# An encoder layer on one core: the reciprocal square roots of its norms move from twelve VectorE instructions to two GpSimd instructions

## The chip, the cores and the metric

The kernel runs on one core of a Trainium2 chip. The metric is the device time of one execution in microseconds (us), smaller is better. Five engines work side by side, each through its own queue of instructions in order: TensorE (PE in the profile, with PEld for its weight loads), VectorE (DVE), ScalarE (ACT), GpSimd (POOL) and SyncE (SP), which here issues the transfers. They wait for one another through semaphores.

## The reference

One layer of an encoder is applied, with the same weights, to two batches: 2048 and 1024 tokens of width 1024. The token mixing has a Fourier half (a two-dimensional DFT) and a half of gating heads (a 128x128 mixing matrix per head); the channel mixing is a gated up-projection to 2 x 2816, a convolution of width 3 over positions, GELU and a down-projection. Around them stand RMS norms, and these are what the change is about:

```python
def _rmsnorm(x, g):
    xf = x.astype(jnp.float32)
    y = xf * lax.rsqrt(jnp.mean(xf * xf, axis=-1, keepdims=True) + EPS)
    return (y * g.astype(jnp.float32)).astype(x.dtype)

def _trunk(x, ...):
    m = _token_mixer(_rmsnorm(x, pre_mix_norm[l]), ...)      # inside: v = _rmsnorm(v, sgu_norm) per head
    x = x + _rmsnorm(m, post_mix_norm[l])
    c = _channel_mixer(_rmsnorm(x, pre_ffn_norm[l]), ...)
    x = x + _rmsnorm(c, post_ffn_norm[l])
```

All arrays are float32, and so are the results.

## The kernel before

The products are done in float32 by splitting each operand into a high part (fp32r, a copy by ScalarE) and the rest (a subtraction by VectorE or GpSimd: `split`), and by three passes over the parts. The large projections use Strassen's scheme in Winograd's form: seven products `p0` to `p6` of twelve matmuls each, made from sums of blocks (`sums`, on GpSimd: s0 to s3) and split operands w0 to w6. The seven products of two tiles of 128 rows are one step.

The program is a list of slots. `at(slot, order, fn)` puts a piece of work into a slot; inside a slot the loads come first, then the preparation for later slots, the matmuls, and what takes the products out of PSUM. At the end all slots are run through in order, and so each engine's queue is fixed: an instruction that waits holds up all that stands behind it on its engine.

The stages, in the order of the slots, are: twelve chunks of 128 tokens times the Fourier columns (`Fourier`, each chunk one slot; tiles xT, xh, xl, pz, z) while the weights of the gating heads get ready (wr, sog); twelve steps of gating heads (`Gate`, seven slots each; names end in g); twelve more Fourier chunks; twelve mixes (`Mix`, four slots each: position DFT with the tables th and tl, output projection, norm, residual, and the norm before the up-projection); 66 steps of the up-projection (`Up`; names end in u); and 36 steps of the down-projection in three groups (`Down`; names end in d), the last of which adds the residual and stores y.

The norms need one number per token (or per token and head), the reciprocal square root of a mean of squares. ScalarE sums the squares into a small tile (ss or vs), 128 partitions by one, two or eight columns. `Rsqrt` turns it into the factor: a first guess by integer operations on the bits of the float, and three rounds of Newton's iteration, together twelve VectorE instructions (L107 to L118). There are 62 of these: r1 for the input's norm (12, into the tile rall; used by `Fourier.out` on VectorE and by `Gate.gelu` on ScalarE), rv per gating step (12, eight columns; used by `vnorm` on VectorE), r2 after each mix (12; used by `residual` on VectorE), r3 before the up-projection (10 of two columns in the mixes and 4 of one column in the first steps of the up-projection; used by ScalarE), r4 in the last down group (11; used by `yout` on VectorE), and rl at the very end.

`Vec` wraps VectorE: behind each large instruction one step of a queued chain is issued, so that a chain is spread over the work of the next slots. Chains with `wait=None` (r1, r2, two-column r3, rl) are issued at once in one piece, since `Rsqrt.__init__` asks for `col(0)`, and `col` issues all that is still queued. The others start in the queue, and whatever is left of them is issued when a user asks for the factor. In the gating steps rv is queued at slot s+6, and its user `vnorm` stands at s+8.

Of the kernel before, what the change touches and what calls it, by code (L numbers as in the profile page):

```python
# [11 lines left out]
F32 = mybir.dt.float32  # L12
# [5 lines left out]
D = 1024  # L18
# [7 lines left out]
# 128-token tiles in processing order: (batch, parity, kt) -> (direct tile, mirrored tile)  # L26
# [7 lines left out]
def tile_trunk(  # L34
# [46 lines left out]
    # Chains of small operations on the vector engine are queued and issued one by one behind  # L81
    # its large operations, so that it doesn't wait for the latency of each.
    queued = []

    class Vec:
        def __getattr__(self, name):
            f = getattr(nc.vector, name)

            def issue(*args, **kw):
                f(*args, **kw)  # L90
                if queued:
                    queued.pop(0)()

            return issue

    vec = Vec()

    class Rsqrt:
        """(ss / n + EPS) ** -0.5 by Newton's iteration, on [128, k]."""

        def __init__(self, ss, k, n, name, wait=None, out=None):
            v = S.tile([128, k], F32, tag=f"nv{k}", name=f"{name}_v")
            yv = S.tile([128, k], F32, tag=f"ny{k}", name=f"{name}_y") if out is None else out
            q = S.tile([128, k], F32, tag=f"nq{k}", name=f"{name}_q")
            tt, ts, stt = nc.vector.tensor_tensor, nc.vector.tensor_scalar, nc.vector.scalar_tensor_tensor
            ops = [lambda: None] * (wait or 0) + [
                lambda: ts(v, ss, 0.5 / n, 0.5 * EPS, op0=ALU.mult, op1=ALU.add),  # L107
                lambda: ts(q.bitcast(I32), v.bitcast(I32), 1, None, op0=ALU.arith_shift_right),
                # the first guess, negative: each of the three iterations changes the sign
                lambda: ts(  # L110
                    yv.bitcast(I32), q.bitcast(I32), -1, 0x5F3759DF - (1 << 22) - (1 << 31),
                    op0=ALU.mult, op1=ALU.add,
                ),
            ]
            ops += 3 * [
                lambda: tt(q, yv, yv, op=ALU.mult),
                lambda: tt(q, q, v, op=ALU.mult),
                lambda: stt(yv, q, -1.5, yv, op0=ALU.add, op1=ALU.mult),  # L118
            ]
            self.done = False  # L120
            queued.extend(ops + [self.end])
            self.y = yv
            if wait is None:
                self.col(0)

        def end(self):
            self.done = True

        def col(self, i):
            while not self.done:  # L130
                queued.pop(0)()
            return self.y[:, i : i + 1]
# [14 lines left out]
    # The program is a list of slots; in each one the loads and splits for later slots are  # L147
    # issued before the products, and what takes the products out of PSUM after them.
# [6 lines left out]
    # Strassen's scheme in Winograd's form for [C11 C12; C21 C22] = [A11 A12; A21 A22] [B11 B12; B21 B22]:  # L155
    # the right operands of the seven products in the order of the products
    B11, B21, T4, T2, T3, T1, B22 = range(7)

    def right_sums(t1, b11, b12, b21, b22, last=True):
        """t1 = T1 and, in place, b12 = T3, b11 = T2, b21 = T4."""  # L160
        nc.gpsimd.tensor_tensor(t1, b12, b11, op=ALU.subtract)
        nc.gpsimd.tensor_tensor(b12, b22, b12, op=ALU.subtract)
        nc.gpsimd.tensor_tensor(b11, b12, b11, op=ALU.add)
        if last:
            nc.gpsimd.tensor_tensor(b21, b11, b21, op=ALU.subtract)

# [28 lines left out]
    class Step:  # L195
        """Two tiles of 128 rows times the right operands of a stage: seven products."""
# [106 lines left out]
    def fold(k):  # L303
        """The rows of the Fourier columns' weights times the DFT over a group's channels."""
        if k % 2 == 0:
            for e in range(2):
                wf[e].append(unit(f"wf{e}{k}", F32R, (128, 2, 512)))
        pf = bank(f"pf{k}")
        for g in range(4):
            nc.tensor.matmul(  # L310
                pf[:, g * 128 : (g + 1) * 128],
                lhsT=wft[k // 2][:, g, (k % 2) * 128 : (k % 2) * 128 + 128],
                rhs=rd, start=True, stop=True,
            )
# [18 lines left out]
    class Stat:  # L333
        """The norm's factors of two chunks of 128 tokens."""
# [11 lines left out]
        def scale(self):  # L346
            pr = self.pr
            ss = S.tile([128, 2], F32, tag="ss1", name=f"ss1_{pr}")
            for j in range(2):
                nc.scalar.activation(self.xc[j], self.xc[j], AF.Square, accum_out=ss[:, j : j + 1])  # L350
            self.r = Rsqrt(ss, 2, D, f"r1_{pr}", out=rall[:, 2 * pr : 2 * pr + 2])

    class Fourier:
        """The Fourier columns of one chunk of 128 tokens."""
# [30 lines left out]
    class Heads(Stage):  # L385
        """The weights of the gating heads; the halves of the columns are v and u."""

        def load(self, q):
            """Blocks 11, 21, 12, 22."""
# [24 lines left out]
    class Gate(Step):  # L414
        """The gating heads of two chunks of 128 tokens."""
# [46 lines left out]
        def vscale(self):  # L462
            self.rv = Rsqrt(self.vs, 8, 128, f"rv{self.nm}", 0)
# [79 lines left out]
    # The Fourier columns come before and after the gating heads, so that each one's  # L543
    # weights get ready while the other's are in use.
# [7 lines left out]
    def begin():  # L552
# [17 lines left out]
        stats[0].scale()  # L570

# [13 lines left out]
    for pr in range(12):  # L585
        if 0 < 2 * pr < NB:
            at(2 * pr - 2, LOAD if pr > 1 else MM + 0.1, stats[pr].load)
            at(2 * pr - 1, PREP + 0.3, stats[pr].scale)
    at(10, STORE, wf_store)
# [13 lines left out]
    for pr in range(12):  # L603
# [3 lines left out]
        if 2 * pr >= NB:  # L607
            at(s - 5, LOAD, stats[pr].load)
            at(s - 3, OUT + 0.5, stats[pr].scale)
        at(s + 1, OUT + 0.2, g.vout, 0)  # L610
        at(s + 5, OUT + 0.2, g.vout, 1)
        at(s + 6, OUT + 0.2, g.vscale)
# [11 lines left out]
    # ------------------------------------------------------------------ position DFT, projection out  # L624
# [49 lines left out]
    def product(o0, o1, aparts, wparts, first=True, last=True):  # L674
        """o0|o1 += the sum over parts of a.T @ w, in three passes."""
# [13 lines left out]
    # the tiles of d_ff: three groups of (first half, second half)  # L689
# [27 lines left out]
    class Side:  # L717
        """z[s] + z[s + S/2], or their difference, of one batch."""
# [21 lines left out]
    class Mix:  # L740
        """One tile of 128 frequencies and the tile of their mirror images."""
# [87 lines left out]
        def centre(self):  # L829
            """The frequency S/2, which has no mirror image."""  # L830
# [74 lines left out]
        def norm(self):  # L905
# [7 lines left out]
            self.r2 = Rsqrt(ss, 2, D, f"r2{nm}")  # L913
# [31 lines left out]
        def rs_again(self, i):  # L945
            vec.tensor_add(self.ss3[:, 0:1], self.ss3[:, 0:1], self.ss3[:, 1:2])
            self.r3 = Rsqrt(self.ss3[:, 0:1], 1, D, f"r3{self.nm}{i}", 0)
# [88 lines left out]
    for i, m in enumerate(mixes):  # L1036
# [26 lines left out]
        at(s + 3 + 4 * (i == 11), OUT + 0.7, m.norm)  # L1063
        at(s + 4 + 6 * (i == 11), OUT + 0.5, m.residual)
# [22 lines left out]
    # ------------------------------------------------------------------ up-projection, conv, gate  # L1087
# [4 lines left out]
    class Up(Step):  # L1092
        """Gate and up of one tile of d_ff; the columns are the even and the odd positions."""
# [116 lines left out]
    # ------------------------------------------------------------------ down-projection  # L1210
# [7 lines left out]
    class Down(Step):  # L1218
        """Two tiles of tokens, one group of d_ff; the columns are the halves of the output's."""
# [31 lines left out]
        def post(self, j):  # L1251
            """The last two steps: as little as possible comes after their last products."""
# [38 lines left out]
        def scale(self):  # L1291
            self.r = Rsqrt(self.ss, 2, D, f"r4{self.nm}", 0)
# [202 lines left out]
```

## Time and profile before

| | |
|---|---|
| median of 3 runs | 2967.51 us (2967.39 to 2967.82) |
| span of the profiled execution | 2965.6 us |
| PE busy | 2722.0 us (92%) |
| DVE busy | 2639.4 us (89%), 3995 instructions |
| ACT busy | 1214.2 us (41%) |
| POOL busy | 1548.3 us (52%), 918 instructions |
| mean granted TensorE clock | 0.966 of full |

The page has no time of the profiled execution other than its span, from the first to the last instruction. A busy share is a mean over stages in which different engines are full, so the rows further down are by stretches and by single steps. The time of an instruction in a row includes what it waits for after its start, as for a port that another engine holds; the time it waits ahead of its start for another instruction's result stands in brackets, with the instruction that ended the wait.

### The profile page before, as it was taken

The numbers are of one execution on the slowest core, as the hardware profiler recorded it, in microseconds if no ns is written. First come the engines' busy times: TensorE is split into PE (matmuls) and PEld (weight loads), VectorE is DVE, ScalarE is ACT, GpSimd is POOL, SyncE is SP. The second block draws the span as 40 slices with busy tenths as digits, with TensorE's granted clock in tenths as the row PEclk, the third lists the DMA queues.
The fourth block names the chain that finished last, engine by engine and source line by source line (L and its number), as shares of the span: only waits on it lengthen the run. The fifth ranks groups of instructions, "written<-read, shape, count | busy, mean of one in ns | idle before, by whom it ended". The sixth has DMA issues, their size and how long they took to land.

```text
span 2965.6 us, 35147 instructions
## 1 busy us (share of the span) xinstructions
PE 2722.0 (92%) x11930; PEld 2192.1 (74%) x11930; DVE 2639.4 (89%) x3995; ACT 1214.2 (41%) x2317; POOL 1548.3 (52%) x918
## 2 busy tenths in 40 slices
PE   8788899988779999998999998999998999999997
PEld 7576777877667777786787776777776887887775
DVE  7988977789799999999999999999999668669999
ACT  5334443454454444444443444344344232224332
POOL 2633411345555555556555556445455337668766
PEclk9899999999889999999999999999998999999999
DMA  8435449456772323252222143122124464566665
GB/s 305 162 130 181 161 167 331 152 187 206 220 241 85 111 96 107 95 175 79 85 86 86 70 151 93 70 80 85 64 96 145 126 204 158 163 202 210 204 191 180
DMA packets 279572, 440.39 MB, mean 149 GB/s; under 512 B 22304, under 2 KB 171296, under 8 KB 279392
## 3 DMA queue, kind: packets, MB, share of 16 engines
q1 hardware_dynamic: 279392, 438.16, 44.1%
q8 instruction: 93, 1.52, 0.2%
q14 instruction: 87, 0.71, 0.1%
HBM read 302.81 MB, written 135.28 MB: 148 GB/s over the span
## 4 chain that ended last, share of the span: by engine, by line
DVE 36%; PE 26%; issue 13%; ACT 3%; DMA 2%; POOL 1%; SPq 0%; DVEq 0%; ACTq 0%; POOLq 0%
DVE t1u L90 8%; DVE t0u L90 4%; PE p3u L234 3%; PE p5u L234 3%; PE p4u L234 3%; DVE uu L90 2%; DVE c21u L90 2%; PE p5d L234 2%; PE p6d L234 2%; PE p4d L234 2%; PE p0d L234 2%; PE p3d L234 2%; PE p2d L234 2%; PE p1d L234 2%; DVE sox L90 2%
## 5 line engine op out<-in xcount | busy, mean ns | idle before, releaser
L1158 POOL TENSOR_TENSOR t0u<-t0u,t1u 128x1024 f32<-128x1024 f32 x66 | 160.0, 2424 | 395.0 <-ACT t0u L1157 394.9
L234 PE MATMUL p3u<-sox,w3u 128*128 128x512 f32 x792 | 208.5, 403 | 22.7 <-DVE w3u L90 21.0
L234 PE MATMUL p0u<-sox,w0u 128*128 128x512 f32 x792 | 201.1, 404 | 25.0 <-ACT w0u L135 13.9
L234 PE MATMUL p6u<-sox,w6u 128*128 128x512 f32 x792 | 200.4, 397 | 9.6 <-DVE w6u L90 9.6
L234 PE MATMUL p2u<-sox,w2u 128*128 128x512 f32 x792 | 198.1, 399 | 10.0 <-ACT w2u L135 5.6
L136 POOL TENSOR_TENSOR w4u<-s2u,w4u 128x512 fp32r<-128x512 f32 x65 | 101.2, 1557 | 202.4 <-ACT w4u L135 198.4
L1157 ACT ACTIVATE t0u<-t0u 128x1024 f32<-128x1024 f32 x66 | 70.1, 1062 | 326.8 <-DVE t0u L90 324.1
L234 PEld LDWEIGHTS p3u<-sox,w3u 128*128 128x128 f32 x792 | 147.1, 191 | 74.0 <-DVE w3u L90 42.3
L234 PE MATMUL p5u<-sox,w5u 128*128 128x512 f32 x792 | 195.0, 395 | 7.4 <-DVE w5u L90 3.8
L234 PEld LDWEIGHTS p0u<-sox,w0u 128*128 128x128 f32 x792 | 154.1, 196 | 61.6 <-ACT w0u L135 16.0
L234 PE MATMUL p4u<-sox,w4u 128*128 128x512 f32 x792 | 192.1, 391 | 2.5 <-DVE w4u L90 2.1
L234 PE MATMUL p1u<-sox,w1u 128*128 128x512 f32 x792 | 191.5, 390 | 2.3 <-DVE w1u L90 2.3
L234 PEld LDWEIGHTS p6u<-sox,w6u 128*128 128x128 f32 x792 | 146.4, 189 | 52.8 <-DVE w6u L90 22.3
L234 PEld LDWEIGHTS p2u<-sox,w2u 128*128 128x128 f32 x792 | 148.5, 191 | 48.9 <-DVE w2u L90 11.2
L234 PEld LDWEIGHTS p5u<-sox,w5u 128*128 128x128 f32 x792 | 150.3, 191 | 41.6 <-DVE w5u L90 5.9
L1109 ACT ACTIVATE t1u<-c21u,cbt,cwt 128x512 f32<-128x512 f32 x66 | 53.9, 817 | 298.3 <-DVE c21u L90 289.1
L90 DVE TENSOR_TENSOR w6u<-s3u,w6u 128x512 fp32r<-128x512 f32 x66 | 155.8, 2360 | 22.1 <-ACT w6u L135 22.1
L234 PEld LDWEIGHTS p4u<-sox,w4u 128*128 128x128 f32 x792 | 149.2, 189 | 34.5 <-DVE w4u L90 2.5
L234 PEld LDWEIGHTS p1u<-sox,w1u 128*128 128x128 f32 x792 | 148.5, 188 | 33.9 <-DVE w1u L90 3.2
L90 DVE SCALAR_TENSOR_TENSOR t1u<-c21u,cwt,t1u 128x511 f32<-128x511 f32 (+4 forms) x220 | 164.7, 772 | 3.1
L242 ACT COPY ud<-p0d 128x512 f32<-128x512 f32 x34 | 20.0, 588 | 346.4 <-PE p0d L234 346.4
L90 DVE SCALAR_TENSOR_TENSOR t1u<-c22u,cwt,t1u 128x511 f32<-128x511 f32 (+4 forms) x220 | 141.5, 668 | 3.1
(363 smaller groups left out, 7724.5 us busy)
## 6 DMA issues: line engine op xcount, KB each, us to landing
ra0u<-w_up SPq DMA_DIRECT2D x66, 512.0 KB, 4.5
ra1u<-w_up SPq DMA_DIRECT2D x66, 512.0 KB, 5.3
g_d<-t0u SPq DMA_DIRECT2D x66, 512.0 KB, 2.9
srx<-xo_d SPq DMA_DIRECT2D x42, 512.0 KB, 6.6
xT<-xT SPq DMA_DIRECT2D x24, 512.0 KB, 8.0
xc<-xc SPq DMA_DIRECT2D x24, 512.0 KB, 5.4
zz<-z_d SPq DMA_DIRECT2D x48, 256.0 KB, 5.5
xr<-x_po SPq DMA_DIRECT2D x24, 512.0 KB, 6.0
```

The costliest lines, as they stand in the source:

```text
L90: f(*args, **kw)
L136: (eng or vec).tensor_tensor(l, src, h.bitcast(F32), op=ALU.subtract)
L234: nc.tensor.matmul(ps, lhsT=w[:, a, k], rhs=op[k][:, b], start=k == 0 and a + b == 0, stop=k == n - 1 and a == 1)
L242: nc.scalar.copy(self.u, p[0])
L1109: nc.scalar.activation(t[:, i], p, AF.Identity, bias=cbt[:, ti : ti + 1], scale=cwt[:, ti, 1:2])
L1157: nc.scalar.activation(ga, ga, AF.Gelu_apprx_tanh)
L1158: nc.gpsimd.tensor_tensor(ga, ga, self.t[1], op=ALU.mult)
```

## The change

`Vec` and its queue go; `vec` is VectorE itself. `Rsqrt` issues two GpSimd instructions at once: mean and epsilon in one affine step, and a power of -0.5 with the exponent from a constant tile. Since they are issued where `Rsqrt` is made, the calls move to slots of their own: `Stat.root` one slot behind the squares (or at the end of the same slot), `vscale` from s+6 to the end of s+7, `Mix.rs2` to the head of the slot of its user `residual`. No other instruction of PE, ScalarE or SyncE is moved.

```diff
@@
-    class Vec:
-        def __getattr__(self, name):
-            f = getattr(nc.vector, name)
-            def issue(*args, **kw):
-                f(*args, **kw)
-                if queued:
-                    queued.pop(0)()
-            return issue
-    vec = Vec()
+    vec = nc.vector
+    power = C.tile([128, 8], F32, name="power")
+    nc.gpsimd.memset(power, -0.5)
@@ class Rsqrt
-            tt, ts, stt = nc.vector.tensor_tensor, nc.vector.tensor_scalar, nc.vector.scalar_tensor_tensor
-            ops = [lambda: None] * (wait or 0) + [
-                lambda: ts(v, ss, 0.5 / n, 0.5 * EPS, op0=ALU.mult, op1=ALU.add),
-                lambda: ts(q.bitcast(I32), v.bitcast(I32), 1, None, op0=ALU.arith_shift_right),
-                lambda: ts(
-                    yv.bitcast(I32), q.bitcast(I32), -1, 0x5F3759DF - (1 << 22) - (1 << 31),
-                    op0=ALU.mult, op1=ALU.add,
-                ),
-            ]
-            ops += 3 * [
-                lambda: tt(q, yv, yv, op=ALU.mult),
-                lambda: tt(q, q, v, op=ALU.mult),
-                lambda: stt(yv, q, -1.5, yv, op0=ALU.add, op1=ALU.mult),
-            ]
...
+            nc.gpsimd.tensor_scalar(v, ss, 1.0 / n, EPS, op0=ALU.mult, op1=ALU.add)
+            nc.gpsimd.tensor_tensor(self.y, v, power[:, :k], op=ALU.pow)
@@ where they are called
+            at(2 * pr - 1, OUT + 0.5, stats[pr].root)
...
+            at(s - 2, OUT + 0.5, stats[pr].root)
...
-        at(s + 6, OUT + 0.2, g.vscale)
+        at(s + 7, OUT + 0.6, g.vscale)
...
+        at(s + 4 + 6 * (i == 11), PREP - 0.1, m.rs2)
```

On VectorE, in the eighth gating step, this stood before the change ahead of the fifth product's operand of the next step (w4g is an operand that TensorE waits for; v2g with rvg_y is `vnorm`):

```order
L90 TENSOR_TENSOR v2g_2758<-ug_2712,p1g_2735 128x512
L116 TENSOR_TENSOR rvg_q<-rvg_y 128x8
L90 COPY gTg_2769<-ptg_2748 128x8x64
L117 TENSOR_TENSOR rvg_q<-rvg_q,rvg_v 128x8
L90 COPY gTg_2769<-ptg_2753 128x8x64
L118 SCALAR_TENSOR_TENSOR rvg_y<-rvg_q,rvg_y 128x8
L116 TENSOR_TENSOR rvg_q<-rvg_y 128x8
L117 TENSOR_TENSOR rvg_q<-rvg_q,rvg_v 128x8
L118 SCALAR_TENSOR_TENSOR rvg_y<-rvg_q,rvg_y 128x8
L90 SCALAR_TENSOR_TENSOR v2g_2510<-v2g_2510,rvg_y,gsg 128x128 x8
L90 TENSOR_TENSOR w4g_2789<-s2g_2621,w4g_2789 128x512
```

and this stands there now:

```order
L401 TENSOR_TENSOR v2g_2579<-ug_2530,p1g_2556 128x512
L491 COPY gTg_2589<-ptg_2569 128x8x64
L491 COPY gTg_2589<-ptg_2574 128x8x64
L437 SCALAR_TENSOR_TENSOR v2g_2353<-v2g_2353,rvg_y,gsg 128x128 x8
L100 TENSOR_TENSOR w4g_2604<-s2g_2444,w4g_2604 128x512
```

All steps of the chain are gone from between these; `vnorm` itself stays where it was.

On GpSimd, in the same gating step, the factor of v and that of a later step's tokens (rall) now stand between the sums of the next step (s2g, s3g) and the sums of the down-projection's weights (wt, wd), which followed one another directly before:

```order
L179 TENSOR_TENSOR s2g_2444<-ra0g_2315,ra1g_2316 128x512
L180 TENSOR_TENSOR s3g_2445<-ra0g_2315,s1g_2443 128x512
L92 TENSOR_SCALAR r_8_v<-ss_8_2439 128x2
L93 TENSOR_TENSOR rall<-r_8_v,power 128x2
L92 TENSOR_SCALAR rvg_v<-vsg_2356 128x8
L93 TENSOR_TENSOR rvg_y<-rvg_v,power 128x8
L125 TENSOR_TENSOR wt_2625<-wd_2546,wd_2545 128x512
```

Four instructions came in; the others keep their order.

On GpSimd, among the first Fourier chunks, the factor of chunks 8 and 9 (r_4) now stands between the two groups of sums of the gating heads' weights (wt, wr):

```order
L127 TENSOR_TENSOR wr_256<-wr_340,wr_256 128x1024
L129 TENSOR_TENSOR wr_303<-wr_256,wr_303 128x1024
L92 TENSOR_SCALAR r_4_v<-ss_4_555 128x2
L93 TENSOR_TENSOR rall<-r_4_v,power 128x2
L125 TENSOR_TENSOR wt_604<-wr_341,wr_257 128x1024
```

Before the change the two groups of four followed one another directly, and r_4 was twelve VectorE instructions ahead of the z of chunk 8.

## Rows read from the trace of the kernel before

**Rows 1.** Stretches: length, busy us (count) of PE, PEld, DVE, ACT, POOL, clock

```profile
0.00:108.00 108.00, 87.04 (x368) 70.10 (x369) 86.34 (x144) 48.86 (x83) 46.02 (x28) 0.94 0.69 261
108.00:430.00 322.00, 281.51 (x1252) 227.75 (x1251) 278.49 (x543) 141.88 (x376) 120.82 (x90) 0.94 0.49 165
...
530.00:920.00 390.00, 322.24 (x1591) 267.31 (x1590) 345.21 (x578) 189.02 (x378) 200.64 (x90) 0.91 0.59 193
...
2700.00:2953.00 253.00, 231.01 (x972) 181.91 (x971) 247.40 (x349) 78.81 (x140) 181.00 (x98) 0.99 0.58 188
```

**Rows 2.** Whom PE waited for: us in all, times, longest

```profile
PE p4g L234 <- DVE w4g L90: 35.3, 11, 6.1
...
PE pq L772 <- DVE tl L90: 18.6, 8, 4.8
PE pz L373 <- DVE xl L90: 15.1, 6, 9.8
PE p0u L234 <- ACT w0u L135: 13.9, 5, 3.4
PE pT L788 <- DVE p4z L90: 11.8, 4, 7.2
PE p0u L234 <- DVE w0u L90: 11.1, 1, 11.1
```

**Rows 3.** Timeline of one gate: start, length, engine, instruction, idle before it

```profile
307.01 2.19 DVE L90 SCALAR_TENSOR_TENSOR v2g<-v2g,rvg_y,gsg 128x128 f32<-128x128 f32 x8
...
309.86 3.45 PE L234 MATMUL p4g<-sog,w4g 128*128 128x512 f32 x10 [3.08 <-DVE w4g L90]
...
322.60 1.29 POOL L161 TENSOR_TENSOR wt<-wd,wd 128x512 f32<-128x512 f32 x1 [11.04 <-DVE u2g L90]
```

**Rows 4.** PE's groups in the gating heads: busy, mean ns, idle before

```profile
L234 PE MATMUL p4g<-sog,w4g 128*128 128x512 f32 x144 | 53.3, 525 | 36.8 <-DVE w4g L90 35.3 <-ACT w4g L135 1.5
...
L234 PE MATMUL p3g<-sog,w3g 128*128 128x512 f32 x144 | 34.6, 389 | 0.0
```

**Rows 5.** VectorE's groups, two steps of the chain, by shape

```profile
L116 DVE TENSOR_TENSOR rvg_q<-rvg_y 128x8 f32<-128x8 f32 x36 | 19.5, 541 | 0.4
...
L117 DVE TENSOR_TENSOR r4d_q<-r4d_q,r4d_v 128x2 f32<-128x2 f32 x33 | 5.3, 161 | 1.1
```

**Rows 6.** Timeline of a step of the last down group

```profile
2813.84 0.65 DVE L107 TENSOR_SCALAR r4d_v<-ss4d 128x2 f32<-128x2 f32 x1
...
2815.01 1.25 DVE L108 TENSOR_SCALAR r4d_q<-r4d_v 128x2 int32<-128x2 int32 x1
...
2818.26 1.28 DVE L90 SCALAR_TENSOR_TENSOR c1d<-c1d,r4d_y,gpo 128x1024 f32<-128x1024 f32 x1
...
2822.67 2.60 PE L234 MATMUL p1d<-sow,w1d 128*128 128x512 f32 x10 [1.54 <-DVE w1d L90]
```

**Rows 7.** Timeline of VectorE in the first Fourier chunks

```profile
69.01 2.36 DVE L107 TENSOR_SCALAR r_v<-ss 128x2 f32<-128x2 f32 x1
...
82.74 0.74 DVE L90 TENSOR_SCALAR z<-pz,rall 128x512 f32<-128x512 f32 x1
```

**Rows 8.** Timeline of the end

```profile
2954.86 1.19 DVE L107 TENSOR_SCALAR rl_v<-ssl 128x2 f32<-128x2 f32 x1
2955.99 1.25 POOL L1303 TENSOR_TENSOR c0d<-c0d,gpo 128x512 f32<-128x512 f32 x1
...
2959.33 0.72 ACT L1310 ACTIVATE c1d<-c1d,rl_y 128x512 f32<-128x512 f32 x1 [5.16 <-DVE rl_y L118]
```

**Rows 9.** GpSimd's groups, one of the smallest and the dearest

```profile
L919 POOL TENSOR_TENSOR es<-es,xr 128x1024 f32<-128x1024 f32 x12 | 44.2, 3687 | 186.1 <-issue 83.4 <-DVE es L90 69.0 <-DMA xo_d<-hT 33.6
...
L1482 POOL MEMSET const-float32-0.0<- 128x1 f32 x1 | 0.1, 104 | 0.2 <-issue 0.2
```

**Rows 10.** Timeline of one mix

```profile
642.84 2.13 DVE L107 TENSOR_SCALAR r_v<-ss 128x2 f32<-128x2 f32 x1
...
649.32 1.15 ACT L931 ACTIVATE xr<-es,r_y 128x1024 f32<-128x1024 f32 x1 [3.10 <-DVE p4z L90]
```

More of the change, by code (lines that the diff above doesn't have):

```diff
@@ L79, in tile_trunk, with __init__ @@
     cbt = const("cbt", cb, [128, 2 * NFT])
-    queued = []
-    class Vec:
-        def __getattr__(self, name):
-            f = getattr(nc.vector, name)
-            def issue(*args, **kw):
-                f(*args, **kw)
-                if queued:
-                    queued.pop(0)()
-            return issue
-    vec = Vec()
+    vec = nc.vector
+    power = C.tile([128, 8], F32, name="power")
+    nc.gpsimd.memset(power, -0.5)
     class Rsqrt:
-        def __init__(self, ss, k, n, name, wait=None, out=None):
+        def __init__(self, ss, k, n, name, out=None):
             v = S.tile([128, k], F32, tag=f"nv{k}", name=f"{name}_v")
-            yv = S.tile([128, k], F32, tag=f"ny{k}", name=f"{name}_y") if out is None else out
-            q = S.tile([128, k], F32, tag=f"nq{k}", name=f"{name}_q")
-            tt, ts, stt = nc.vector.tensor_tensor, nc.vector.tensor_scalar, nc.vector.scalar_tensor_tensor
-            ops = [lambda: None] * (wait or 0) + [
-                lambda: ts(v, ss, 0.5 / n, 0.5 * EPS, op0=ALU.mult, op1=ALU.add),
-                lambda: ts(q.bitcast(I32), v.bitcast(I32), 1, None, op0=ALU.arith_shift_right),
-                lambda: ts(
-                    yv.bitcast(I32), q.bitcast(I32), -1, 0x5F3759DF - (1 << 22) - (1 << 31),
-                    op0=ALU.mult, op1=ALU.add,
-                ),
-            ]
-            ops += 3 * [
-                lambda: tt(q, yv, yv, op=ALU.mult),
-                lambda: tt(q, q, v, op=ALU.mult),
-                lambda: stt(yv, q, -1.5, yv, op0=ALU.add, op1=ALU.mult),
-            ]
[L120 to L127, printed above, removed]
+            self.y = S.tile([128, k], F32, tag=f"ny{k}", name=f"{name}_y") if out is None else out
+            nc.gpsimd.tensor_scalar(v, ss, 1.0 / n, EPS, op0=ALU.mult, op1=ALU.add)
+            nc.gpsimd.tensor_tensor(self.y, v, power[:, :k], op=ALU.pow)
         def col(self, i):
-            while not self.done:
-                queued.pop(0)()
             return self.y[:, i : i + 1]
@@ L350, in scale, with root @@
                 nc.scalar.activation(self.xc[j], self.xc[j], AF.Square, accum_out=ss[:, j : j + 1])
-            self.r = Rsqrt(ss, 2, D, f"r1_{pr}", out=rall[:, 2 * pr : 2 * pr + 2])
+            self.ss = ss
+        def root(self):
+            pr = self.pr
+            self.r = Rsqrt(self.ss, 2, D, f"r1_{pr}", out=rall[:, 2 * pr : 2 * pr + 2])
     class Fourier:
@@ L462, in vscale @@
         def vscale(self):
-            self.rv = Rsqrt(self.vs, 8, 128, f"rv{self.nm}", 0)
+            self.rv = Rsqrt(self.vs, 8, 128, f"rv{self.nm}")
         def vnorm(self, j):
@@ L570, in begin @@
         stats[0].scale()
+        stats[0].root()
     def fourier_events(s, f):
@@ L912, in norm, with rs2 @@
                 nc.scalar.activation(scr, self.x1[i], AF.Square, accum_out=ss[:, i : i + 1])
-            self.r2 = Rsqrt(ss, 2, D, f"r2{nm}")
+            self.ss2 = ss
+        def rs2(self):
+            self.r2 = Rsqrt(self.ss2, 2, D, f"r2{self.nm}")
         def residual(self):
@@ L946, in rs_again @@
             vec.tensor_add(self.ss3[:, 0:1], self.ss3[:, 0:1], self.ss3[:, 1:2])
-            self.r3 = Rsqrt(self.ss3[:, 0:1], 1, D, f"r3{self.nm}{i}", 0)
+            self.r3 = Rsqrt(self.ss3[:, 0:1], 1, D, f"r3{self.nm}{i}")
         def norm_again(self, i):
@@ L1291, in scale @@
         def scale(self):
-            self.r = Rsqrt(self.ss, 2, D, f"r4{self.nm}", 0)
+            self.r = Rsqrt(self.ss, 2, D, f"r4{self.nm}")
         def closing_load(self):
```

## The prediction

> **What bounds the kernel now.** I read the profile in this order: busy time in stretches, to see which engine fills each stage; the list of whom TensorE waited for; then the timeline around the longest of those waits.
>
> The stretches [rows 1] are, in the program's order: the first Fourier chunks (to 108 us), the gating heads (108 to 430), the last Fourier chunks, the position DFT with the output projection, called the mixes here (530 to 920), the up-projection (to 2290) and the down-projection, whose last group runs from 2700. The reader is to compare each stretch's length with PE's and DVE's busy time. In the gating heads PE works 281.5 of 322 us at a mean clock of 0.94, in the mixes 322.2 of 390 at 0.91, in the last down group 231.0 of 253. In two of these three VectorE is the fuller engine beside it (345.2 of 390; 247.4 of 253).
>
> The list of waits [rows 2] says who is late: nearly every long wait of PE ends with a VectorE instruction that prepares a left operand or a table (w4g, tl, xl, w1d). PE is the engine that has to be full, and VectorE, which runs its queue in order, is what keeps it from that.
>
> What stands in that queue ahead of w4g is the chain of the norm and its users [rows 3]: the eight instructions that scale v can start at 307.01 only, when the chain's last step is done, they run for 2.19 us, then comes w4g, and PE goes on with p4g at 309.86. PE waited 3.08 us there and 35.3 us so in 11 of the 12 gates [rows 2]. Each wait costs again afterwards: the p4g matmuls take 525 ns in the mean and the same matmuls of p3g 389 [rows 4], so the 144 of p4g are 53.3 − 34.6 = 18.7 us dearer than those of p3g, in a stretch where the granted clock is below full.
>
> **The change part by part.** Twelve VectorE instructions go from each of 62 places: 12 for the tokens (r1, tile rall), 12 for the gating heads (rvg), 12 after the mixes (r2), 14 before the up-projection (r3), 11 for the output (r4d) and one at the end (rl). In the clear one step takes 161 ns [rows 5]; with its gap it is 0.2 us (ten steps between the end of r4d_q at 2816.26 and c1d at 2818.26 [rows 6]), so twelve are 2.4 us. Beside a busy GpSimd they take more: a 128x8 square takes 541 ns in the mean [rows 5], and one r1 chain runs from 69.01 to the z behind it at 82.74, 13.7 us, its first step alone 2.36 us for two columns [rows 7].
>
> The Trainium skill says why (SBUF — State Buffer, "Who interferes with whom"): a GpSimd instruction and a VectorE one with two SBUF inputs take turns at a shared port, each blocking the other for a whole instruction. The 1.19 us of rl_v, beside GpSimd's products of 1.25 us, agrees [rows 8].
>
> Added are 124 small GpSimd instructions. No row shows a power. From below, the smallest GpSimd row is 104 ns, from above the dearest group is 3.69 us for 1024 columns [rows 9]. I take 0.2 us for the affine step and 0.6 us for the power, near the lower end, since two to eight columns are all there is. GpSimd has room: 120.8 us busy of 322 in the gating heads, 200.6 of 390 in the mixes, 181.0 of 253 at the end [rows 1].
>
> Now the sum, by stretches.
>
> Gating heads. GpSimd stands idle for 11.04 us before wt at 322.60 [rows 3], and the new pair comes just ahead of wt, so it can be done around 322; before the change the scaling of v asked for it a period after 307.01, at 333.8 (322 us for 12 gates: 26.8 each), after it perhaps 5 us earlier. So nothing waits unless the power takes some 7 us. VectorE's queue is shorter by 2.4 us a gate at least, by 6.5 if all twelve steps are like the squares (12 × 541 ns), w4g comes that much earlier, and the wait of 3 us goes with the slow matmuls behind it. To be had are 35.3 + 18.7 = 54 us; I take 46, since p4g will be late now and then for ACT's part. Range 20 to 60.
>
> First Fourier chunks. PE waited 15.1 us for xl, 9.8 of it at once, behind the 13.7 us chain [rows 2, 7]. After the change z waits for GpSimd's r_4 instead, which stands behind four sums of 128x1024; r_v, which would wait for one of those, got through at 71.4 (69.01 + 2.36), so z may come some 10 us before 82.74. I take 8; range 0 to 15.
>
> Mixes. There are 22 chains (12 r2, 10 r3). PE waits for tl 18.6 us, for p4z 11.8, for the first w0u 11.1 [rows 2]. In the trace one r3 chain, begun at 642.84, holds ACT's xr until 649.32 [rows 10]. But r3 on GpSimd stands behind the two sums ds and es of the next mix, so xr hardly comes earlier; what gains is what VectorE does meanwhile. Of these 41.5 us I take 24; from −10 (ACT waits longer for r3) to 45.
>
> First up-projection steps. Four r3 chains of one column; ACT's norm waits for them and PE for ACT, 13.9 us [rows 2]. I take 8; range 0 to 14. The other 62 steps hold no norm and stay.
>
> Last down group. The chain and w0d between its steps take from 2813.84 to 2818.26 [rows 6], 4.4 us of which w0d is 0.6. PE then waits 1.54 for w1d; in this stretch PE is idle 253 − 231 = 22 us. GpSimd has the new pair right behind its c0d sum, some 4 us before VectorE asks. I take 13; range 0 to 20.
>
> The end. From rl_v to the first use 4.47 us [rows 8]; the pair on GpSimd waits for the two products with the gain that now run beside the chain, to about 2957.2, then 0.8. I take 1; range −3 to 2.
>
> Sum: 46 + 8 + 24 + 8 + 13 + 1 = 100 us. The profiled span is 2965.6, so 2865.6. The median of the runs, 2967.5, lies 1.9 us above the span, the only measure of what lies around it: 2867.5 us.
>
> **The rivals.**
>
> First, the waiting stays. The time of a VectorE step that is a wait for GpSimd does not vanish: the next one with two SBUF inputs meets the same GpSimd instruction, and 124 new ones take turns as well. Then a chain frees its own 2.4 us less 0.8 for the new pair, 1.6. Gating heads: 18 chains (12 rvg, 6 r1), 29 us; mixes: 22 chains, half of 35 on the path, 17; last group: 11 chains, 18 us, of which I let 5 reach PE. With nothing elsewhere that is 51, or 2916.5 us. For it speaks rl_v's 1.19 beside a 1.25 us product [rows 8]; against it that GpSimd is idle for two thirds of the gating heads [rows 1]. The Trainium skill has this caution too (Perfetto Trace Analysis, "Optimizing Scalar/DVE Operations"): since the two engines share a port, moving work between them "might not help". By that alone the time would stay; the 11.04 us of idle GpSimd at the very place does not bear it out there.
>
> Second, the other side: the power is dear. In the mixes r2 is asked for by the very next VectorE instruction, and r3 by ACT, so 22 times its price p is paid in full in place of 2.4 us. The other terms give 100 − 24 = 76, so from p = 2.4 + 76/22 = 5.9 us on the kernel is slower; at 8 us it loses 22 × 5.6 = 123 there and 12 in the gating heads (1 us over the slack of 7), 2967.5 − 76 + 135 = 3026.5 us. No row shows a price; the dearest GpSimd group at 3.69 us for 1024 columns [rows 9] speaks against 8 us for two.
>
> Third, more than I think: PE becomes full in the gating heads and the mixes. There it is idle 40.5 and 67.8 us [rows 1]; with all the 41.5 of the mixes and 58 in the heads the sum grows by 30, to 2838.
>
> **How the numbers follow.** Forecast (2845 to 2895) 0.63, more (2815 to 2845) 0.15, waiting stays (2895 to 2945) 0.13, dear power 0.07, no change 0.02. The range of 8 in 10 takes the forecast, most of the fast case and most of the first rival: 2825 to 2935. A measurement can tell some 0.2%, 6 us, from no change. Faster 0.91, same 0.02, slower 0.07.
>
> **What would show it.** Right: no wait of p4g for w4g beyond 10 us in all, the heads' stretch down from 322 to about 275, the power below 1 us, xl's 9.8 us gone, p1d's waits halved. Wrong: VectorE's w and tl rows longer than now by what the chains freed (first rival); new waits of VectorE or ACT for the power, first of all in the mixes (second).

## The result

The changed kernel takes 2834.89 us (median of 4 runs, 2832.35 to 2838.39) against 2967.66 us for the kernel before in the same session: ratio 0.9549, 95% interval 0.9536 to 0.9563. That is 132.8 us less, where 100 were forecast; the range of 2825 to 2935 holds it, though outside the forecast's own band of 2845 to 2895. One later execution, the profiled one of the first run with wd's sums moved, was granted a clock of 0.57 and took 4321.63 us; it is left out of all times.

The profile after, busy time by engine (us, share of the span, instructions):

```profile
span 2833.3 us, 34584 instructions
PE 2679.7 (95%) x11930; PEld 2165.4 (76%) x11930; DVE 2435.1 (86%) x3251; ACT 1213.1 (43%) x2317; POOL 1640.8 (58%) x1043
```

PE's idle time went from 2965.6 − 2722.0 = 243.6 us to 2833.3 − 2679.7 = 153.6, so 90.0 us of the gain are waits that are gone. The other 42.3 us are the same 11930 matmuls done faster, at a mean granted clock that rose from 0.966 to 0.983. VectorE has 744 instructions fewer, 62 times 12, and 204 us less to do.

The stretches of [rows 1], in the same columns (length, PE, PEld, DVE, ACT, POOL, clock, DMA share, GB/s):

```profile
0.00:108.00 108.00, 92.70 (x400) 73.83 (x400) 69.92 (x78) 54.10 (x94) 57.91 (x43) 0.98 0.76 280
108.00:430.00 322.00, 308.41 (x1465) 255.42 (x1465) 250.21 (x363) 148.43 (x377) 171.68 (x130) 0.98 0.58 200
530.00:920.00 390.00, 358.13 (x1732) 295.64 (x1731) 323.50 (x387) 211.09 (x423) 255.87 (x154) 0.96 0.62 203
```

The same windows now hold more of the program; the heads' window, in which PE works 308.4 of 322 us, ends 55.5 us into the last Fourier chunks. In the heads' own stage PE works 266.6 of 284.2 us at a mean clock of 0.98, before the change 281.7 of 321.7 at 0.94.

For where the time went I took the first starts of each stage's matmuls in both traces (p0g, pz of the last Fourier chunks, pq, p0u, p0d, the last p0d matmul, the end) and subtracted. Lengths in us:

| stage | before | after | gain | forecast |
|---|---|---|---|---|
| to the first p0g: first Fourier chunks | 104.4 | 90.3 | 14.1 | 8 |
| gating heads | 321.7 | 284.2 | 37.5 | 46 |
| last Fourier chunks | 73.5 | 74.5 | −1.0 | 0 |
| mixes | 365.2 | 326.6 | 38.6 | 24 |
| up-projection | 1395.5 | 1368.2 | 27.3 | 8 |
| down-projection to the last p0d | 667.7 | 657.0 | 10.7 | 13 |
| from the last p0d to the end | 37.6 | 32.5 | 5.1 | 1 |
| sum | 2965.6 | 2833.3 | 132.3 | 100 |

Whom PE waits for, after (us in all, times, longest), answering to [rows 2]:

```profile
PE p4g L198 <- DVE w4g L100: 11.3, 11, 2.1
PE p1d L198 <- DVE w1d L100: 6.5, 5, 2.6
PE p0u L198 <- DVE w0u L100: 4.7, 3, 4.0
PE pq L743 <- DVE tl L100: 4.1, 3, 3.3
PE pz L341 <- DVE xl L100: 3.5, 5, 1.2
PE p0u L198 <- ACT w0u L99: 2.4, 1, 2.4
```

Every wait that was named fell: w4g 35.3 to 11.3, tl 18.6 to 4.1, xl 15.1 to 3.5 with a longest of 1.2, w0u behind ScalarE 13.9 to 2.4; p4z's 11.8 is not in the list any more.

What the new instructions cost, GpSimd's groups after (busy, mean ns, idle before):

```profile
L93 POOL TENSOR_TENSOR r_y<-r_v,power 128x2 f32<-128x2 f32 x22 | 20.4, 929 | 1.8
L93 POOL TENSOR_TENSOR rvg_y<-rvg_v,power 128x8 f32<-128x8 f32 x12 | 19.7, 1642 | 1.0
L93 POOL TENSOR_TENSOR r4d_y<-r4d_v,power 128x2 f32<-128x2 f32 x11 | 7.8, 708 | 0.9
L92 POOL TENSOR_SCALAR rvg_v<-vsg 128x8 f32<-128x8 f32 x12 | 2.4, 196 | 74.5 <-ACT sqg L423 74.5
```

The power takes 0.71 us for two columns in the last down group, 0.93 in the mixes, and 1.64 for eight: dearer than the 0.6 I took, far below the 5.9 from which the second rival decides. The affine step's 0.2 us is right.

One gate after the change, answering to [rows 3] (start, length, engine, instruction, idle before). VectorE's and PE's part first:

```profile
268.06 5.20 DVE L437 SCALAR_TENSOR_TENSOR v2g<-v2g,rvg_y,gsg 128x128 f32<-128x128 f32 x8
273.18 0.68 DVE L100 TENSOR_TENSOR w4g<-s2g,w4g 128x512 fp32r<-128x512 f32 x1
273.92 2.58 PE L198 MATMUL p4g<-sog,w4g 128*128 128x512 f32 x10 [0.60 <-DVE w4g L100]
```

GpSimd in the same stretch and up to the next factor:

```profile
261.49 1.29 POOL L125 TENSOR_TENSOR wt<-wd,wd 128x512 f32<-128x512 f32 x1
...
267.84 1.29 POOL L177 TENSOR_TENSOR s0g<-ra1g 128x512 f32<-128x512 f32 x1
269.21 1.29 POOL L178 TENSOR_TENSOR s1g<-s0g,ra0g 128x512 f32<-128x512 f32 x1
270.46 1.34 POOL L179 TENSOR_TENSOR s2g<-ra0g,ra1g 128x512 f32<-128x512 f32 x1
...
282.81 0.20 POOL L92 TENSOR_SCALAR rvg_v<-vsg 128x8 f32<-128x8 f32 x1 [4.35 <-ACT sqg L423]
283.09 1.64 POOL L93 TENSOR_TENSOR rvg_y<-rvg_v,power 128x8 f32<-128x8 f32 x1
```

The factor of the next gate is there at 284.7, some 6.5 us before its users start at 291.26. The users themselves are dearer: the eight took 2.19 us [rows 3] and take 5.20, while s0g, s1g and s2g run from 267.84 to 271.8 beside them. GpSimd, which had stood idle for 11.04 us ahead of wt, now has seven of its eight sums in one run that ends where VectorE's small instructions stand. In the ten gates that have such sums the eight users take 5.20 to 5.88 us. The last two gates have none, and there the same instructions take 2.19 us again:

```profile
360.04 2.19 DVE L437 SCALAR_TENSOR_TENSOR v2g<-v2g,rvg_y,gsg 128x128 f32<-128x128 f32 x8
```

In the gate shown PE still waits 0.60 us there, and the p4g and p3g groups that answer to [rows 4] are nearer to each other:

```profile
L198 PE MATMUL p4g<-sog,w4g 128*128 128x512 f32 x144 | 41.4, 428 | 14.3 <-DVE w4g L100 11.3 <-ACT w4g L99 3.1
...
L198 PE MATMUL p3g<-sog,w3g 128*128 128x512 f32 x144 | 35.8, 397 | 2.1 <-DVE w3g L100 2.1
```

The end, answering to [rows 8], with the sum ssl that the factor is made from; before the change it stood at

```profile
2954.20 0.62 DVE L90 TENSOR_TENSOR ssl<-ssl 128x2 f32<-128x2 f32 x1 [0.85 <-ACT sq1d L1302]
```

and after it the end is

```profile
2822.88 0.62 DVE L1282 TENSOR_TENSOR ssl<-ssl 128x2 f32<-128x2 f32 x1 [0.85 <-ACT sq1d L1277]
2826.00 0.19 POOL L92 TENSOR_SCALAR rl_v<-ssl 128x2 f32<-128x2 f32 x1
2826.28 0.71 POOL L93 TENSOR_TENSOR rl_y<-rl_v,power 128x2 f32<-128x2 f32 x1
2827.02 0.72 ACT L1285 ACTIVATE c1d<-c1d,rl_y 128x512 f32<-128x512 f32 x1 [4.17 <-POOL rl_y L93]
```

From rl_v to the first use it is 1.02 us, before 4.47; but rl_v now starts later, behind GpSimd's two products. From ssl to the first use it is 4.14 us, before 5.13.

### The profile page after: what moved, and what is told of

It reads as the page before. It is cut to its first block, busy times and chain, and to the rows that moved or that the text cites. A ratio compares the mean times of both kernels' runs of the same rounds, so it can differ in the third digit from the quotient of the medians.

```text
span 2833.3 us, 34584 instructions
## 1 busy us (share of the span) xinstructions
PE 2679.7 (95%) x11930; PEld 2165.4 (76%) x11930; DVE 2435.1 (86%) x3251; ACT 1213.1 (43%) x2317; POOL 1640.8 (58%) x1043
## 5 line engine op out<-in xcount | busy, mean ns | idle before, releaser
L198 PEld LDWEIGHTS p3u<-sox,w3u 128*128 128x128 f32 x792 | 147.4, 191 | 74.5 <-DVE w3u L100 42.3
L198 PE MATMUL p0u<-sox,w0u 128*128 128x512 f32 x792 | 192.7, 392 | 7.1 <-DVE w0u L100 4.7
L100 DVE TENSOR_TENSOR w6u<-s3u,w6u 128x512 fp32r<-128x512 f32 x66 | 159.2, 2412 | 21.1 <-ACT w6u L99 20.7
```

The source lines that it names most:

```text
L100: (eng or vec).tensor_tensor(l, src, h.bitcast(F32), op=ALU.subtract)
L198: nc.tensor.matmul(ps, lhsT=w[:, a, k], rhs=op[k][:, b], start=k == 0 and a + b == 0, stop=k == n - 1 and a == 1)
```

## The experiments

The first four put the pair on GpSimd for one kind of norm alone and leave VectorE's chain for the others. All four have this edit, with other kinds in the list, and the move of the call that belongs to the kind. Times are medians of all executions; what a stage gains is read from the profiled ones, where the kernel before has a span of 2965.6 us.

```diff
+            kind = "late" if k == 1 else name[:2]
...
+            if kind in ('rv',):
...
+                nc.gpsimd.tensor_scalar(v, ss, 1.0 / n, EPS, op0=ALU.mult, op1=ALU.add)
+                nc.gpsimd.tensor_tensor(self.y, v, power[:, :k], op=ALU.pow)
+                return
...
```

**rv alone** (twelve factors in the gating heads).

> Only the twelve chains of the gating heads (rv) go to GpSimd, at the slot they have in the changed kernel; all others stay chains on VectorE. Theory A (each group of chains held up its own stage, one after the other): the whole gain of that stage, some 37 us, 2930 us, with p4g's waits for w4g down from 35 to about 11. Theory B (the gain is a joint one, by less traffic on the port that VectorE and GpSimd share): clearly less, 2945 or more.

Measured: 2934.55 us (2933.61 to 2935.21) against 2970.95 before in that session, ratio 0.9878 (0.9864 to 0.9893): 36.4 us. The heads' stage is 36.0 us shorter, no other stage changes by more than 2.2: theory A. Its forecast of the waits missed: p4g still waits 18.1 us for w4g, not 11.

**r2 and the two-column r3** (22 factors in the mixes; list `('r2', 'r3')`).

> Only the 22 two-column chains of the mixes (r2, r3) go to GpSimd. Theory A: the mixes' whole gain of some 40 us, 2927 us. Theory B: half of that or less, 2947 or more.

Measured: 2928.31 us (2925.57 to 2932.09), ratio 0.9859 (0.9843 to 0.9874): 42.6 us. The profiled executions differ by 36.4 us, 36.4 in the mixes and 2.9 in the up-projection, with small losses elsewhere: theory A.

**The four one-column r3** of the first up-projection steps (list `('late',)`).

> Only the four one-column chains of r3 in the first up-projection steps go to GpSimd, at the slot they had. The two profiles differ by 6.0 us at each of four steps there. Theory A: those 24 us, 2943.5. Theory B: under 10, as the prediction had it from PE's waits for w0u (8), 2958 or more.

Measured: 2944.34 us, ratio 0.9915 (0.9898 to 0.9931): 26.6 us for four chains, 23.0 of it in the up-projection's stage: theory A.

**r1, r4 and rl** (list `('r1', 'r4', 'rl')`).

> Only r1, r4 and rl go to GpSimd (24 chains: input norm, last down group, end). Theory A: 14 us in the first Fourier chunks, 11 in the last group, 5 at the end: 30 in all, 2937.5, and with the three others 37 + 40 + 24 + 30 = 131 of the 132.8 us. Theory B: the four sum to less than 110.

Measured: 2943.10 us, ratio 0.9908 (0.9893 to 0.9923): 27.9 us. By stages: the first Fourier chunks 14.2, the down-projection 11.3, the end 5.1; the heads, where six r1 pairs joined GpSimd while rv's chain stayed, got 4.7 us longer.

The four gains add up to 36.4 + 42.6 + 26.6 + 27.9 = 133.5 us, against the whole change's 132.8. That is closer than the runs can tell: each gain is known to 4 or 5 us, and all four are taken from the same runs of the kernel before. By the spans of the profiled executions they add up to 32.8 + 36.4 + 24.1 + 21.5 = 114.8 of 132.3 us; in the heads to 30.4 of 37.5. Neither count is under the 110 of theory B, but up to some 18 us may come only from the parts together. Two of them, the mixes and the four late chains, hold what the forecast had too small.

**The four late chains issued in one piece.** The kernel before, with nothing on GpSimd. The queued chain was spread over the large instructions of the step, each of its steps taking its turn behind one of them:

```diff
-            self.r3 = Rsqrt(self.ss3[:, 0:1], 1, D, f"r3{self.nm}{i}", 0)
+            self.r3 = Rsqrt(self.ss3[:, 0:1], 1, D, f"r3{self.nm}{i}")
```

> The kernel before, with the four late one-column chains issued in one piece where they are made and not step by step behind VectorE's large instructions; still twelve VectorE instructions each. Theory Q (their cost is the lateness of the factor: the steps stand in the queue behind other work, ScalarE waits for the last one, and what stands behind ScalarE's instruction waits too): most of the 24 us, 2945. Theory V (their cost is VectorE's time for twelve instructions): nothing or a loss, 2967 or more.

Measured: 2953.42 us against 2972.22 before, ratio 0.9947 (0.9928 to 0.9967): 18.8 us of the 26.6, 16.4 of them in the up-projection's stage. So most of this part was not VectorE's time but a late factor. The kernel before shows it in ScalarE's list of waits (us in all, times, longest):

```profile
ACT xa L950 <- DVE r_y L118: 33.6, 4, 8.4
```

The scaling of xa stood 8.4 us in ScalarE's queue in each of four steps, and all that stood behind it came late. In the trace after it waits for nothing:

```profile
1039.01 1.15 ACT L924 ACTIVATE xa<-xa,r_y 128x1024 f32<-128x1024 f32 x1
```

By the starts of `uu`, the copy of p0u out of PSUM, the two traces part by 5.6, 6.0, 6.0 and 6.0 us at just these four steps. At the others the distance changes by some 1 us to and fro, but for 3.4 us the other way at the second step.

**The change, with VectorE's twelve instructions left in as idle work.** Beside each pair stand twelve small instructions on VectorE that nothing reads:

```diff
...
+            q, w = (S.tile([128, k], F32, tag=f"n{t}{k}", name=f"{name}_{t}") for t in "qw")
+            vec.tensor_scalar(q, half1[:, :k], 0.5, None, op0=ALU.mult)
+            vec.tensor_scalar(w, half1[:, :k], 0.5, None, op0=ALU.mult)
+            for _ in range(3):
+                vec.tensor_tensor(q, w, w, op=ALU.mult)
+                vec.tensor_tensor(q, q, half1[:, :k], op=ALU.mult)
+                vec.scalar_tensor_tensor(w, q, -1.5, w, op0=ALU.add, op1=ALU.mult)
+            vec.tensor_scalar(q, w, 0.5, None, op0=ALU.mult)
```

> The changed kernel, with a chain of twelve VectorE instructions of the same kinds and sizes issued beside each GpSimd pair, on a constant; nobody reads what it makes. Theory V (VectorE's time for the chains was the cost): most of the gain goes, 2910 or more. Theory Q (the cost was that others waited for the chain's result): most stays, under 2870.

Measured: 2926.69 us, ratio to before 0.9855 (0.9838 to 0.9872), 92 us over the changed kernel. Its waits of PE:

```profile
PE p4g L208 <- DVE w4g L110: 24.0, 11, 2.6
PE pz L351 <- DVE xl L110: 15.8, 8, 5.9
PE p1d L208 <- DVE w1d L110: 15.2, 12, 2.5
```

The waits for w4g, xl and w1d come back, in part or whole (11.3, 3.5 and 6.5 without the idle work; 35.3, 15.1 and 20.7 in the kernel before), though every factor still comes from GpSimd. So small instructions in VectorE's queue do cost PE's time: the prediction's main step. How much of the gain they are is told by the stages of the profiled executions. The idle work takes back 13.5 of the 14.1 us in the first Fourier chunks, 21.9 of 37.5 in the heads, 16.2 of 38.6 in the mixes and 11.1 of 27.3 in the up-projection. Behind that it takes 26.7 us where the change had brought 15.8: it costs more there than the chains did, perhaps as it stands in one piece and not step by step. So some 78 of the 132 us are shown to be VectorE's queue, and more than half of what the mixes and the up-projection gain is not. The idle instructions read a constant and make nothing that others wait for; the late chains above (16.4 us) are a part of the rest, and the wait for r3 in the mixes, further down, is another.

**Four powers in place of one**, three unread:

```diff
...
+            e = S.tile([128, k], F32, tag=f"ne{k}", name=f"{name}_e")
+            for _ in range(3):
+                nc.gpsimd.tensor_tensor(e, v, power[:, :k], op=ALU.pow)
```

> The changed kernel with four powers at each place in place of one (three go to a tile that nobody reads): the factor comes 3 x 0.71 = 2.1 us later for two columns and 3 x 1.64 = 4.9 us later for eight. Rival of the dear power: the delay is paid in full at the 22 chains of the mixes, 22 x 2.1 = 47 us, and nowhere else: 2882. Slack theory: GpSimd has time ahead of most users: under 15 us, 2850 or less.

Measured: 2944.59 us, ratio 0.9919 (0.99 to 0.9938): 110 us over the changed kernel, more than twice what was expected. The heads lose 52.5 us, the mixes 31. In the heads I had claimed room of 7 us for the power, and three more of them take 5. One gate of this run, VectorE:

```profile
303.65 8.54 DVE L440 SCALAR_TENSOR_TENSOR v2g<-v2g,rvg_y,gsg 128x128 f32<-128x128 f32 x8
312.11 0.68 DVE L103 TENSOR_TENSOR w4g<-s2g,w4g 128x512 fp32r<-128x512 f32 x1
```

and GpSimd:

```profile
300.58 1.89 POOL L96 TENSOR_TENSOR rvg_y<-rvg_v,power 128x8 f32<-128x8 f32 x1
302.44 1.29 POOL L128 TENSOR_TENSOR wt<-wd,wd 128x512 f32<-128x512 f32 x1
303.81 1.34 POOL L129 TENSOR_TENSOR wd<-wd,wd 128x512 f32<-128x512 f32 x1
...
310.47 1.31 POOL L182 TENSOR_TENSOR s2g<-ra0g,ra1g 128x512 f32<-128x512 f32 x1
```

The factor is done at 302.5 and its first user starts at 303.65: in this gate nothing waits for it. But six of GpSimd's eight sums run beside the eight users, which then take 8.54 us, and w4g stands behind them. In the heads the price of the power is paid by whoever meets the work behind it. In the mixes the factor itself is late as well: ScalarE's scaling xr waits 41.0 us for it, 17.2 in the changed kernel. Neither theory of the expectation holds.

Three runs follow that up; all change the order in the changed kernel alone.

**The eight users behind w4g.**

```diff
-        at(s + 8, OUT + 0.5, g.vnorm, 0)
-        at(s + 8, OUT + 0.5, g.vnorm, 1)
+        at(s + 9, PREP + 0.3, g.vnorm, 0)
+        at(s + 9, PREP + 0.3, g.vnorm, 1)
```

> The changed kernel (2834.9 us) with the eight users of v's factor one place later: behind the preparation of w4g in VectorE's queue, not ahead of it. Theory A: what PE still waits for in the heads (11.3 us for w4g) is the eight users standing ahead of w4g, 5.2 us a gate in place of 2.2. With them behind, w4g comes earlier, p4g's waits go to nearly nothing, and the heads' stretch loses those 11 us: about 2823 us. Rival B: the wait only moves to the next operand in the queue (w5g, or ug for p5g's place in PSUM), as the eight users still take 5 us somewhere: within 4 us of 2835.

Measured: 2842.29 us, ratio to before 0.9575 (0.956 to 0.9589), no gain over the changed kernel's 0.9549. Theory A falls. In the heads (3.7 us longer) it is as rival B says: the wait has moved to the next operand, and the users are hardly cheaper (664 ns in the mean of the twelve gates, 684 in the changed kernel; the 0.71 us of the expectations leaves a gate out). With 7 us more than the changed kernel the time itself is outside B's 4 us.

```profile
PE p5g L198 <- DVE w5g L100: 12.5, 10, 2.5
```

Another 6.1 us stand in the up-projection's stage and arise in its first four steps: PE waits 11.0 us at once for w0u there, 4.0 in the changed kernel. Why this w0u is late stays open.

**wd's sums behind the gate's own.**

```diff
-        at(SB + 7 * i + 3, PREP, wd_sums, i)
+        at(SB + 7 * i + 5, PREP, wd_sums, i)
```

> The changed kernel with GpSimd's four sums for the down-projection (wt, wd) two slots later, behind the gate's own sums s0g to s3g and not ahead of them. Theory C (collision): the eight users of v's factor take 0.71 us each in place of 0.35 because wt, wd and s0g to s2g run beside them; with wd later, s0g to s2g are done before the users start, the users fall to some 0.35 us, p4g's waits go from 11.3 to below 3 us, and the kernel comes to about 2824 us. Rival D: the users are slow because of their own data or their own form, whatever GpSimd does: their mean stays at 0.7 us and the time at 2835.

Measured: 2825.66 us (2821.33 to 2826.38), ratio 0.9515 (0.9499 to 0.9531). Its trace is that of the execution that is left out, so the kernel ran once more:

> The same kernel as e9_wd_later again, whose three timed runs came to 2821 to 2826 us but whose trace was taken at a granted clock of 0.57 and can't be read against the others. Theory C (collision): the eight users of v's factor fall from 0.71 to about 0.35 to 0.45 us each, p4g waits for w4g for under 3 us in all, the heads' stretch is some 9 us shorter than the changed kernel's 284.2, and the time is about 2825 us. Rival D: the users still take 0.7 us, and the gain comes from elsewhere in the program.

Measured: 2824.62 us (2821.67 to 2827.37) against 2969.38 before, ratio 0.951 (0.9497 to 0.9523), below the changed kernel's interval of 0.9536 to 0.9563. It beats both kernels. VectorE, then GpSimd, in one gate:

```profile
257.46 3.26 DVE L437 SCALAR_TENSOR_TENSOR v2g<-v2g,rvg_y,gsg 128x128 f32<-128x128 f32 x8
260.64 0.68 DVE L100 TENSOR_TENSOR w4g<-s2g,w4g 128x512 fp32r<-128x512 f32 x1
```

```profile
257.96 1.29 POOL L179 TENSOR_TENSOR s2g<-ra0g,ra1g 128x512 f32<-128x512 f32 x1 [0.61 <-ACT sqg L423]
261.46 1.62 POOL L180 TENSOR_TENSOR s3g<-ra0g,s1g 128x512 f32<-128x512 f32 x1 [2.21 <-DVE w4g L100]
263.03 2.28 POOL L125 TENSOR_TENSOR wt<-wd,wd 128x512 f32<-128x512 f32 x1
```

In this gate one sum (s2g) meets the users, not three, and they take 3.26 us; PE's waits for w4g are 0.9 us in all. The heads' stage is 269.6 us, 14.6 below the changed kernel's; 3.6 of that are given back in the mixes and 2.3 in the up-projection. Theory C holds, though the users' mean, 496 ns, stays above the 350 to 450 expected.

**Both moves at once.**

> Both moves at once, the users of v's factor behind w4g and wd's sums behind the gate's own. If A and C are two ways to the same 11 us, it is no better than the better of the two, about 2823; if the users of 2 us now meet wd's sums behind w4g instead (wd then runs where they stand), their mean is back at 0.7 us, but nothing waits for it, and the time is the same 2823. Below 2815 it would show that VectorE's time is worth something beyond p4g's waits there.

Measured: 2834.37 us, ratio 0.9549 (0.9533 to 0.9565): no better than the changed kernel, and worse than wd's move alone. The users of v's factor are cheaper than in the changed kernel (461 ns in the mean) but stand ahead of w5g and vlg, and behind these w6g comes late: PE waits for it 7.1 us in 8 gates; the heads' stage is 280.4 us. The expectation missed: moving the users costs what moving wd brings.

**r2 alone** (the kernel before, list `('r2',)`).

> The kernel before with only r2 (the twelve factors after the mixes) on GpSimd; r3 stays on VectorE. The two together gave about 41 us, where 24 were forecast. Theory E (VectorE's time, chain by chain): the stretch gains as its chains go, 12 of 22, so about 22 us: 2949. Theory F: the gain is r3's, since ACT's xr and with it the next mix waited 48.5 us for p4z and the rest behind that chain: r2 alone gives 10 us or less, 2960. Theory G: it is r2's, since r2 is asked for by the very next VectorE instruction: 32 us or more, 2938.

Measured: 2951.11 us against 2968.61, ratio 0.994 (0.9926 to 0.9955): 17.5 us, 15.2 in the mixes; so theory E's 22 is the nearest, and r3 brings the other 42.6 − 17.5 = 25 us with fewer chains, ten. ScalarE's wait for the second scaling of the mixes (xr) tells why. In the kernel before:

```profile
ACT xr L931 <- DVE p4z L90: 48.5, 8, 11.7
```

with r2 alone on GpSimd:

```profile
ACT xr L943 <- DVE p4z L90: 45.1, 8, 8.9
```

and in the changed kernel:

```profile
ACT xr L905 <- POOL r_y L93: 17.2, 9, 4.0
```

The list names p4z, the last instruction of VectorE before xr starts; its 48.5 us stay when r2's chain goes and fall to 17.2 when r3's goes. PE's wait for this xr (9.0 us in the kernel before, 8.2 with r2 alone) is 0.9 in the run with r2 and r3. The seventh of these scalings shows where the time lies. Before the change es is GpSimd's last sum ahead of the factor, and the chain follows:

```profile
732.21 2.71 POOL L824 TENSOR_TENSOR es<-es,os 128x1024 f32<-128x1024 f32 x1
735.39 1.24 DVE L107 TENSOR_SCALAR r_v<-ss 128x2 f32<-128x2 f32 x1
743.58 0.16 DVE L118 SCALAR_TENSOR_TENSOR r_y<-r_q,r_y 128x2 f32<-128x2 f32 x1
```

and at the same scaling after it:

```profile
666.21 2.72 POOL L795 TENSOR_TENSOR es<-es,os 128x1024 f32<-128x1024 f32 x1
669.29 0.71 POOL L93 TENSOR_TENSOR r_y<-r_v,power 128x2 f32<-128x2 f32 x1
```

The chain ended 8.8 us behind es, as six of its steps took 1.1 to 1.2 us each beside GpSimd's next sums; the pair ends 1.1 us behind es. In six of the ten mixes that have this factor the chain was 1.8 to 3.3 us behind es, in the other four 6.7 to 8.8.

## Why the prediction was right, and where its sizes were off

**The bound and the mechanism: right.** VectorE's queue in order was what kept PE from being full. The idle chain shows it for some 78 of the 132 us, and each part alone shortens the stage that it was said to shorten. For the rest the runs show a second way, which the prediction had put too small: others waited for the chain's result, in the four late chains and in r3. What makes up the heads' rest is not shown run by run. That the total came so near is in part luck: the heads brought 8.5 us less than forecast, the mixes and the up-projection 33.9 more.

**Heads, 46 forecast, 37.5 measured (36.4 with rv alone).** The step that fell short is that w4g comes earlier by all that the chain frees, so that its wait of 3 us goes. The factor comes in time, as said, but GpSimd's sums now run beside the users, 5.20 us for 2.19. It is VectorE that came earlier and hardly GpSimd that came later. wt, the first of the sums, starts as soon as VectorE's u2g is done, both before the change (first line, the gate of [rows 3]) and after it (second line, u2g in the gate shown):

```profile
294.84 1.29 POOL L161 TENSOR_TENSOR wt<-wd,wd 128x512 f32<-128x512 f32 x1 [11.88 <-DVE u2g L90]
260.68 0.68 DVE L411 TENSOR_TENSOR u2g<-ug,p6g 128x512 f32<-128x512 f32 x1
```

u2g ends at 261.36 and wt starts at 261.49, so the pair ahead of it costs some 0.1 us. But the users start 6.6 us behind wt (268.06) where they started 12.2 us behind it (307.01): the chain's steps between are gone, and the last two of these had themselves run beside s1g and s2g, 1.2 us each. So 11.3 us of w4g's 35.3 are left. Only with four powers does the pair push the sums: there wt starts 5.5 us behind u2g's end. This is the first rival's mechanism in one place: a wait for the shared port that moves. The rule I had named beside it (the Trainium skill, SBUF — State Buffer, "Who interferes with whom": the two engines take turns for whole instructions) is borne out by these users, 347 ns each before, 684 after, 1032 with four powers. The 1.19 us of rl_v, which the prediction set beside the rule, are no case of it as it was put there: rl_v has one input, ssl. Of the 18.7 us of slow p4g matmuls 53.3 − 41.4 = 11.9 came back; with the 24.0 us of waits for w4g that is nearly all of the stage's 37.5.

**First Fourier chunks, 8 forecast, 14.1 measured:** inside its range of 0 to 15; xl's wait of 9.8 us is gone as said. The r1 pairs cost elsewhere: 4.7 us in the heads where they came alone.

**Mixes, 24 forecast, 38.6 measured.** The step that failed is "xr hardly comes earlier". I had set r3's pair behind ds and es, which is right, and thought that it would so be as late as VectorE's chain; ScalarE's wait in fact fell from 48.5 to 17.2 us. The mix that I had read [rows 10] is one in which the chain ended 1.8 us behind es; in four of the ten it ended 6.7 to 8.8 us behind.

**First up-projection steps, 8 forecast, 27.3 measured, outside the range of 0 to 14.** I took PE's waits for w0u behind ScalarE, 13.9 us, as all that could be had. ScalarE's own list of waits has 33.6 us at this place: the engine in the middle was the row to read, since its late work reaches PE by more than one operand. Four times 6 us went.

**Last down group and end, 13 and 1 forecast, 10.7 and 5.1 measured:** w1d's waits fell from 20.7 us to 6.5, more than halved. The pair of the end waits for GpSimd's two products, as said, and from ssl to the first use 1.0 us is gained, the forecast; the other 4.1 us of the last stage lie ahead of ssl.

**The rivals.** The dear power didn't come, as the price is 0.71 to 1.64 us; four powers, some 2.8 to 6.6 us, cost 110 us but still didn't make the kernel slower than before (2944.59 against 2972.22). Its point of decision, 5.9 us for two columns, was not reached. "The waiting stays" holds for about a fifth: by the sums of their rows the chains took 285.7 us of VectorE, and the rows that stay take 60.4 us more, 32.3 of it the eight users; its sign, longer w and tl rows, shows 3.9 us in all. "More than I think" gave 2838 for the heads and the mixes filled up; the time came out there, but by another way: the heads fell short, and the up-projection and the mixes brought it. The caution that moving work between the two engines "might not help" (the Trainium skill, Perfetto Trace Analysis, "Optimizing Scalar/DVE Operations") held for part of the heads, and not for the whole: 4.5% were gained.

**The signs.** Of those named for "right", xl's 9.8 us and the halving of p1d's waits came. The others were just missed: 11.3 us for w4g where 10 was the limit, 284.2 us for the heads where about 275 was said, 1.64 us for the power of eight columns where 1 was.

## What to carry to other kernels

Where an engine that works in order keeps the bound engine waiting, small instructions in its queue can cost more than their own time (26.6 us for four late chains, whose 48 steps would take some 10 us at the 0.2 us each that they take in the clear), and moving them to an engine with room pays; read the waits of the engine in the middle too, not just those of the bound one, for a late factor holds up all that is queued behind its user. After such a move look at what now runs side by side: here VectorE, freed of the chain, reached its small two-input instructions while GpSimd's sums were still running, and moving four of those sums two slots later was worth another 10 us.

## What the runs showed of the hardware that was not expected

- GpSimd's power of -0.5 took 0.71 us for 128x2 (0.93 in the mean of the mixes) and 1.64 us for 128x8 in its groups, the affine step 0.20 us for 128x8.
- Eight 128x128 instructions on VectorE (v2g, with the factor per partition and the gain as inputs) took 2.19 us with GpSimd idle, 3.26 beside one sum of 128x512, 5.20 beside three and 8.54 beside six: about 1 us more for each sum. w4g, a subtraction of 128x512 right behind them with no sum beside it, takes 0.68 us in all three gates shown.
